# Another opening for a two-layer encoder trunk: x loaded ahead of c, c multiplied as 48 rows in fp32r, and a new order of the work

## The chip, the core and the metric

One Trainium2 chip, one core of it. The metric is the device time in microseconds of one execution of the program. The kernel before has been timed three times: 724.77, 724.97 and 725.40 us; its profiled execution took 725.12 us.

## The reference

Two layers, a sequence of 256 tokens of width 1024, everything in float32. Each layer is modulated by a vector `c`: shift, scale and gate come out of a product with `w_ada` (1024 x 6144). Cut to what matters here:

```python
c_act = jax.nn.silu(c)
for l in range(DEPTH):                                       # 2
    ada = c_act @ w_ada[l] + b_ada[l]
    sh1, sc1, gt1, sh2, sc2, gt2 = split(ada)                # six pieces of 1024
    h = rms(x, g_mix[l]) * (1.0 + sc1) + sh1
    parts = split(h @ w_in[l])                               # 1024 -> 5120
    qa, ka = axial_rope(rms(qa, q_norm_a[l]), ...), ...      # gains per head dimension
    y_a = gqa_attention(qa, ka, va) @ w_branch_a[l]
    y_b = dilated_attention(qs, ks, vs) @ w_branch_b[l]
    x = x + gt1 * ((gate_a * y_a + gate_b * y_b) @ w_out[l])
    h2 = rms(x, g_mlp[l]) * (1.0 + sc2) + sh2
    x = x + gt2 * (square(relu(h2 @ w_ff1[l])) @ w_ff2[l])
```

So before the first product with `w_in` can run, the kernel needs: x, its root mean square and its transpose; silu(c); the first 128 columns of shift and scale, which are rows of `w_ada` reduced against silu(c); and the first 128 rows of `w_in`.

## The kernel before

**Tiling.** x lies in SBUF as two halves of 128 tokens (t = 0, 1). The width 1024 is cut into eight blocks of 128, k = 0 to 7. Weights come as tiles of 128 x 1024 float32 (512 KB) through a ring of seven buffers `wr`. A weight tile is split into two fp32r parts, a high part written by ScalarE (ACT) and the remainder written by VectorE (DVE); so is h. A product is then three fp32r matmuls: high by high, low by high, high by low. A "plain" product is a single float32 matmul on the unsplit tiles, which the profile shows as two MATMUL rows of 512 columns.

**Order of the work.** Instructions are not issued as the code calls them. A class `Plan` records every operation, and at the end plays them through with a table of costs: each engine takes the operation that is due first among those that are ready. `OPEN`, `CFG`, `FIRST`, `COLD`, `FILL` and the like are its constants: `OPEN["loads"]` and `OPEN["steps"]` give the order of loads and of steps in the opening, `OPEN["eng"]` which engine (a for ACT, d for DVE) takes each step's copies and norms, and `seq0` and `seq1` the order in which later pieces are recorded. As all operations are issued by one helper, every row of the profile has the same line; tiles tell them apart.

**The opening** is what is done before and during the products of h with the first 128-row blocks of `w_in`:

- `c_in` holds c as 8 rows of 128 beside an 8 x 8 identity, padded to 128 rows with zeros. `step_c` makes silu(c) (tanh on ACT, a product on DVE), and eight plain float32 matmuls with a picked identity column broadcast each of the 8 rows to all partitions; two ACT copies write `c_act`, 128 x 1024.
- `xin` holds an identity, biases, gains, rotary tables and the two halves of x, loaded by two transfers, x0 and x1.
- `step_a` reduces the first two `w_ada` tiles against `c_act` (DVE, the rows CUSTOM_DVE_ANT_0 of the profile, ISA in the order). `first_sh_sc` then adds bias and gain with two small DVE rows, for each k.
- `step_x` makes the two sums of squares of a half, the power -1/2 on GpSimd (POOL), the normalised half `xn` and its transposes `xT` through PE. `step_t` makes the rotary tables of the first layer on PE.
- `step_h` and `step_m` are the first stage: h of block k = 0, and its products with the tiles `wx` and `wy`, of which `OPEN["plain"]` names those that are plain. Then follow k = 1 to 7 in a loop, each with two `w_ada` tiles, two weight tiles and 24 fp32r matmuls.
- `keep_warm(n)` issues matmuls on a zeroed tile `warm`, n units of 128 columns; `WARM` of them stand first on PE.

Of the kernel before, what the change touches and what calls it, by code (L numbers as in the profile page):

```python
# [12 lines left out]
F32 = mybir.dt.float32  # L13
# [7 lines left out]
P = 128  # L21
D = 1024
# [12 lines left out]
  post0=(5, 2, 1, 0), s2k=9, ahead=1, last="k",  # L35
  hk=2,
  ada_f0=[2, 3, 11, 2, 0, 1, 0, 8, 1], ada_f1=[1, 0, 0, 0, 0, 0, 0, 0, 0],
  seq0="w v v w a w c3 c4 a w w v w a v u a w w w w w u w w w b w b w w v w u w y w w w y w y y w".split(),
  seq1="w u w c4 v w w w w w a w u w c3 w v a a w c5 w w u w w c2 w a w y w y y w y w w u w b w w w b v w v w".split())
WR = 7  # L40
NB8 = 16
WARM = 5
# [4 lines left out]
FIRST = 500.0  # L47
# [6 lines left out]
X0 = 128 + 16 + 128 + 256  # L54
OPEN = dict(
    loads="x0 x1 a0 a1 wx wy",
    steps="C T1 F0 X0 A X1 T0 F1 Wy H0 Wx H1 My0 Mx0 Mx1 My1",
    eng=dict(c0="a", c1="a", ss00="d", ss01="a", ss10="d", ss11="a", xn00="a", xn01="d", xn10="a",
             xn11="a", xT00="a", xT01="a", xT10="d", xT11="a", t00="a", t01="a", t10="a", t11="a",
             h0="d", h1="a", i0="d", i1="a"),  # L60
    plain="y0 y1",
    shift={})
COLD = 5200.0
FILL = (6000.0, 3), (8500.0, 4)
# [92 lines left out]
class Plan:  # L157
# [101 lines left out]
    def record(self, e, op, a, k):  # L259
# [6 lines left out]
        o["also"], o["then"], o["soon"] = [], None, self.soon and e == "SP"  # L266
# [22 lines left out]
    def cost(e, op, outs, ins, k):  # L289
# [18 lines left out]
        if e == "SP":  # L308
# [26 lines left out]
    def links(self):  # L335
        last = {}
        for o in self.ops:
# [6 lines left out]
            for kind, fs in (("r", o["r"]), ("w", o["w"])):  # L344
                for name, space, p0, p1, m in fs:
                    for j, jk, q0, q1, jm in last.get(name, ()):
# [7 lines left out]
                        late = not same or o["e"] == "SP" or (o["e"] != "PE" and kind == "r")  # L354
# [46 lines left out]
    def due(self, seq, at=None):  # L401
# [12 lines left out]
        for o in reversed(self.ops):  # L414
            i = o["i"]
            d = due[i]
            lat = 3500 if o["e"] == "SP" else o["lat"]
# [12 lines left out]
    def run(self, due):  # L430
# [8 lines left out]
        free["SP"] = 0.0  # L439
        pipe = [0.0]  # L440
        dve_port, held_port, last_cut = 0.0, (0.0, 0.0), ""
        chain, pending = False, None
# [34 lines left out]
        def expect(i, depth=0):  # L477
            z = 0.0
            for j, how in ops[i]["need"].items():
                if ops[j]["e"] == "SP":  # L480
                    z = max(z, landed.get(j, 1e18))
                    continue
# [63 lines left out]
        while count < n:  # L546
            moved = False
            for e in ORDERED:
# [15 lines left out]
                if pick is None and seen[e] == state[0] and e not in again:  # L564
                    if e == "DVE" and pending is not None:
                        held_port = enter(*pending, t)
                        pending = None
# [47 lines left out]
                if e == "DVE" and pending is not None and (  # L615
                    pick is None or not chain or not ops[pick]["port"] or ops[pick]["occ"] < 100.0 or t > free[e] + 30.0
                ):
# [18 lines left out]
                if e == "DVE":  # L636
# [4 lines left out]
                    chain = o["port"] and slow == 0.0 and "reduce" not in o["op"]  # L641
                elif e == "POOL":
# [1242 lines left out]
```

## Time and profile before

| What | Before |
|---|---|
| Median of three executions | 724.97 us |
| Profiled execution, its own time | 725.12 us |
| Its span | 723.3 us |
| PE busy | 718.4 us (99%) |
| DVE, ACT busy | 587.6 us (81%), 466.3 us (64%) |
| First matmul on a weight tile | 12.70 us |
| Read from HBM | 178.66 MB |

The profile lists times from the start of the span. A row of the timeline is a run of like instructions on one engine: when the first began, how long the run lasted, what it wrote and read, and in brackets how long the engine had stood idle ahead of it and what ended that. PEld is the loading of weights into the array, which runs beside PE. SPq is the queue from which transfers are issued. In a table of windows each line gives, for a stretch of time, the busy time of the engines and the number of their instructions, then granted clock, share of the DMA engines and GB/s.

### The profile page before, as it was taken

The page shows a single profiled execution, that of the slowest core. Times are in us where ns is not written, and L with a number is a line of the kernel's source. Part 1 is how long each engine was busy: PE and PEld are TensorE (multiplying, and loading weights), DVE is VectorE, ACT ScalarE, POOL GpSimd, SP SyncE. Part 2 cuts the span into 40 slices and gives each one's busy share as a digit, 9 for nine tenths or more (in the row PEclk, how much of TensorE's full clock was granted, in tenths as well). Part 3 has the DMA queues.
Part 4 walks back from the last instruction along what each step waited for, and adds up shares of the span by engine and source line. Part 5 has one row for each costly group of instructions (what it writes and reads, how often), then busy time and mean ns, then how long its engine had stood idle before and what let it go on. Part 6 is the DMA issues. An engine that isn't in the chain of part 4 may idle for free.

```text
span 723.3 us, 10610 instructions
## 1 busy us (share of the span) xinstructions
PE 718.4 (99%) x3860; PEld 597.2 (83%) x3860; DVE 587.6 (81%) x919; ACT 466.3 (64%) x791; POOL 69.6 (10%) x60
## 2 busy tenths in 40 slices
PE   9999999999999999999999999999999999999998
PEld 6788888788888888888888888878788888888887
DVE  6999999999999986594799999797899755456643
ACT  7569678965764766653565598658848766545640
POOL 0007640000100040000032201010000000000000
PEclk9999999999999999999999999999999999999999
DMA  9998668997499997596565687967376965576101
GB/s 349 408 401 270 193 203 295 348 373 243 142 350 406 381 359 278 183 325 233 175 221 207 213 328 269 338 226 280 122 258 199 344 207 159 172 229 211 52 0 59
DMA packets 50868, 180.95 MB, mean 250 GB/s; under 512 B 5728, under 2 KB 6784, under 8 KB 50816
## 3 DMA queue, kind: packets, MB, share of 16 engines
q1 hardware_dynamic: 50816, 180.28, 70.7%
q8 instruction: 30, 0.49, 0.3%
q14 instruction: 22, 0.18, 0.1%
HBM read 178.66 MB, written 1.06 MB: 248 GB/s over the span
## 4 chain that ended last, share of the span: by engine, by line
PE 98%; DMA 1%; SPq 0%; issue 0%; DVE 0%
PE ps L721 98%; DMA wr<-in_w_y 1%; SPq L721 0%; DVE xin L721 0%
## 5 line engine op out<-in xcount | busy, mean ns | idle before, releaser
L721 DVE TENSOR_TENSOR w<-wr,w 128x1024 fp32r<-128x1024 f32 x234 | 282.3, 1229 | 44.7 <-ACT w L721 44.3
L721 ACT ACTIVATE w<-wr 128x1024 fp32r<-128x1024 f32 x234 | 241.5, 1056 | 81.8 <-PE ps L721 38.9
L721 PE MATMUL ps<-w,hT 128*128 128x512 f32 x1032 | 246.4, 395 | 0.0
L721 PEld LDWEIGHTS ps<-w,hT 128*128 128x128 f32 x1032 | 190.3, 188 | 41.5 <-DVE hT L721 1.7
L721 PE MATMUL ps<-w,hid 128*128 128x512 f32 (+1 forms) x780 | 176.0, 385 | 0.0
L721 PEld LDWEIGHTS ps<-w,hid 128*128 128x128 f32 x780 | 143.1, 188 | 28.3
L721 PE MATMUL ps<-hT,w 128*128 128x512 f32 (+1 forms) x896 | 158.5, 337 | 0.0
L721 PEld LDWEIGHTS ps<-hT,w 128*128 128x128 f32 x896 | 139.4, 190 | 18.7
L721 DVE CUSTOM_DVE_ANT_0 s2k<-wr,c_act 128x1024 bf16<-128x1024 f32 x96 | 116.1, 1227 | 0.0
L721 ACT ACTIVATE s2k<-ps 128x256 f32<-128x256 f32 (+3 forms) x108 | 45.4, 440 | 81.0 <-PE ps L721 75.3
L721 DVE TENSOR_TENSOR s2k<-ps,s2k 128x256 f32<-128x256 f32 x56 | 22.8, 419 | 32.5 <-ACT s2k L721 32.5
L721 PE MATMUL ps<-w,mT 128*128 128x512 f32 x192 | 45.6, 393 | 0.0
L721 ACT ACTIVATE s2k<-s2k 128x512 f32<-128x512 f32 (+1 forms) x62 | 38.6, 623 | 9.2 <-DVE s2k L721 8.3
L721 PEld LDWEIGHTS ps<-w,mT 128*128 128x128 f32 x192 | 35.5, 188 | 7.4 <-ACT mT L721 0.2
L721 POOL TENSOR_TENSOR rstd<-rstd,half 128x8 f32<-128x8 f32 (+1 forms) x20 | 30.1, 1509 | 87.8 <-DVE rstd L721 87.7
L721 POOL TENSOR_TENSOR ss<-ss,half 128x1 f32<-128x1 f32 x8 | 11.1, 1383 | 261.7 <-DVE ss L721 254.6
L721 DVE TENSOR_TENSOR hid<-s2k,hid 128x512 fp32r<-128x512 f32 x28 | 20.1, 719 | 19.8 <-ACT hid L721 19.7
L721 ACT ACTIVATE pr<-pr,st 128x256 f32<-128x256 f32 (+1 forms) x64 | 32.3, 558 | 0.8 <-DVE st L721 0.8
L721 DVE TENSOR_TENSOR s2k<-ps,gtb 128x512 f32<-128x512 f32 (+1 forms) x18 | 11.7, 658 | 18.4 <-PE ps L721 18.4
L721 PEld LDWEIGHTS ps<-xin,s2k 128*128 128x128 f32 x180 | 20.9, 141 | 6.3 <-DVE s2k L721 1.2
L721 PE MATMUL ps<-xin,s2k 128*128 128x128 f32 x180 | 26.0, 274 | 0.0
L721 POOL TENSOR_TENSOR s2k<-s2k,tabs 128x256 f32<-128x256 f32 (+1 forms) x20 | 20.2, 1031 | 57.8 <-ACT s2k L721 51.5
(109 smaller groups left out, 505.0 us busy)
## 6 DMA issues: line engine op xcount, KB each, us to landing
wr<-in_w_ff SPq DMA_DIRECT2D x120, 512.0 KB, 4.9
wr<-in_w_ada SPq DMA_DIRECT2D x96, 512.0 KB, 5.7
wr<-in_w_gate SPq DMA_DIRECT2D x32, 512.0 KB, 4.8
wr<-in_w_qkv SPq DMA_DIRECT2D x24, 512.0 KB, 5.3
wr<-in_w_x SPq DMA_DIRECT2D x16, 512.0 KB, 5.2
wr<-in_w_out SPq DMA_DIRECT2D x16, 512.0 KB, 5.3
wr<-in_w_y SPq DMA_DIRECT2D x8, 512.0 KB, 6.7
wr<-in_w_ba SPq DMA_DIRECT2D x8, 512.0 KB, 6.1
```

The costliest lines, as they stand in the source:

```text
L721: getattr(self.real[o["e"]], o["op"])(*map(real, o["a"]), **{n: real(z) for n, z in o["k"].items()})
```

## The change

1. **Loads.** x is issued first on SyncE's queue (SP), with x1 ahead of x0; c is issued from ACT's queue, as its first instruction. x1 carries the columns the first layer's opening needs (biases and gains `early`, head gains, both rotary tables). All other biases and gains are a transfer `small` of 64 KB that is planned near 50 us. The identity is made by GpSimd. The `w_ada` and weight tiles of the first stage come in the order a1, a0, wy, wx in place of a0, a1, wx, wy.
2. **c.** It has 48 rows: 8 rows of c, zeros up to row 32, the 8 rows again, zeros. ACT writes all as fp32r, DVE replaces rows 32 to 47 by the remainder of that rounding, and eight fp32r matmuls over 48 rows take the place of eight plain ones. DVE instead of ACT copies the result to `c_act`.
3. **Modulation.** Bias and gain enter the reduction as its start value and its scale, as columns read from SBUF; the constants 0.5 and 0.0 stood there. Of the two small rows behind each pair one is left (`one_more`).
4. **First stage.** Only wx by the half t = 1 is plain; before, both halves by wy were. PSUM tiles of the stage are allotted where they are first used, not all at once.
5. **Constants and orders.** `WARM` 8 in place of 5, other fills, other planner constants (with a rule for GpSimd's wait on DVE), and new `post0`, `ada_f0`, `seq0`, `seq1`, so that the order differs to the end of the program.

```diff
-  seq0="w v v w a w c3 c4 a w w v w a v u a w w w w w u w w w b w b w w v w u w y w w w y w y y w".split(),
+  seq0="a w v w v w w c4 c3 a w u v w a a w v u w w w w w w b w w b u w w w v y w w y w w w y w y".split(),
-WARM = 5
+WARM = 8
+CR = 48
-    loads="x0 x1 a0 a1 wx wy",
-    steps="C T1 F0 X0 A X1 T0 F1 Wy H0 Wx H1 My0 Mx0 Mx1 My1",
+    loads="x1 x0 a1 a0 wy wx",
+    steps="Wy C X0 X1 T0 T1 F0 A H1 Mx1 F1 H0 Wx My0 Mx0 My1",
-    plain="y0 y1",
+    plain="x1",
-COLD = 5200.0
-FILL = (6000.0, 3), (8500.0, 4)
+COLD = 6650.0
+FILL = (6000.0, 3), (10500.0, 1)
...
+    pool.memset(ident, 0.0)
+    pool.affine_select(
+        out=ident, in_=ident, compare_op=ALU.not_equal, fill=1.0, base=0, pattern=[[-1, P]], channel_multiplier=1
+    )
...
-        dve.tensor_tensor_reduce(junk, raw, c_act, 0.5, 0.0, ALU.mult, ALU.add, col)
+        dve.tensor_tensor_reduce(junk, raw, c_act, *ends(l, w, s, k), ALU.mult, ALU.add, col)
+    def ends(l, w, s, k):
+        ks = slice(k, k + 1)
+        if s < 2 and (l, w) == (0, 0):
+            return (0.5, early[:, 0, ks]) if s == 0 else (early[:, 2, ks], 0.0)
+        return (g_col[:, l, w, ks], 0.0) if s == 1 else (0.5, b_col[:, l, w, s, ks])
+    def one_more(k):
+        sc = shg[0, 0][:, 1, k : k + 1]
+        dve.tensor_tensor(sc, sc, early[:, 1, k : k + 1], op=ALU.add)
-    def first_sh_sc(k):
...
-        dve.tensor_scalar(sc, sc, g_col[:, 0, 0, k : k + 1], gb[:, k : k + 1], op0=ALU.mult, op1=ALU.add)
-        dve.tensor_tensor(sh, sh, b_col[:, 0, 0, 0, k : k + 1], op=ALU.add)
...
     with plan.first():
-        sp.dma_start(c_in, a["c"])
+        act.dma_start(c_in[:CR], a["c"])
...
+        with plan.rush():
+            act.activation(c_sig, z, AF.Tanh, scale=0.5)
+            dve.scalar_tensor_tensor(z, c_sig, 1.0, z, op0=ALU.add, op1=ALU.mult)
+            act.activation(c_f[:CR], c_in[:CR], AF.Copy)
+            dve.tensor_tensor(c_f[low, :P], c_row[low], f32(c_f[low, :P]), op=ALU.subtract)
...
-                    ps[:, k * P : (k + 1) * P], pick[:, kk : kk + 1].to_broadcast([P, P]), c_row,
+                    ps[:, k * P : (k + 1) * P], c_f[:CR, P + kk : P + kk + 1].to_broadcast([CR, P]), c_f[:CR, :P],
...
-    r["x0"] = con(np.concatenate([np.eye(P, dtype=np.float32), b_col, g, g0, g0, cs[0], x[0]], 1))
-    r["x1"] = con(np.concatenate([x[1], cs[1]], 1))
+    r["small"] = con(np.concatenate([b_col, g], 1))
+    r["x0"] = con(x[0])
+    r["x1"] = con(np.concatenate([x[1], b_col[:, :16], g[:, :8], g0, g0, cs[0], cs[1]], 1))
```

SP's queue at the start of the program. Before:

```order
L721 DMA c_in<-in_c 128x136
L721 DMA xin<-in_x 128x1552
L721 DMA xin<-in_x 128x1280
L721 DMA wr_83<-in_w_ada 128x1024
L721 DMA wr_84<-in_w_ada 128x1024
L721 DMA wr_85<-in_w_x 128x1024
L721 DMA wr_86<-in_w_y 128x1024
```

Now:

```order
L723 DMA xin<-in_x 128x1576
L723 DMA xin<-in_x 128x1024
L723 DMA wr_86<-in_w_ada 128x1024
L723 DMA wr_87<-in_w_ada 128x1024
L723 DMA wr_88<-in_w_y 128x1024
L723 DMA wr_89<-in_w_x 128x1024
```

c has left the queue (48 x 136 words of it now stand on ACT's), x has 2600 words a row in place of 2832, and wx is last.

DVE between the sums of squares (`ss`) and the first h (`s2k` out of `xT` and `shg`, which is h of one half). Before:

```order
L721 SCALAR_TENSOR_TENSOR ss_104<-ss_104 128x1
L721 TENSOR_SCALAR s2k_101<-xin,ss_103 128x512
L721 ISA s2k_93,shg_80<-wr_83,c_act 128x1024
L721 ISA shg_80 128x1
L721 ISA s2k_94,shg_80<-wr_84,c_act 128x1024
L721 ISA shg_80 128x1
L721 TENSOR_TENSOR shg_80<-shg_80,xin 128x1
L721 TENSOR_SCALAR shg_80<-shg_80,xin 128x1
L721 TENSOR_SCALAR s2k_98<-xT,shg_80 128x128
```

Now (ss_106 is of the half t = 1, ss_107 of t = 0):

```order
L723 COPY c_act<-ps_76 128x512
L723 SCALAR_TENSOR_TENSOR ss_106<-ss_106 128x1
L723 COPY c_act<-ps_77 128x512
L723 TENSOR_SCALAR s2k_104<-xin,ss_106 128x512
L723 SCALAR_TENSOR_TENSOR ss_107<-ss_107 128x1
L723 ISA s2k_98,shg_83<-wr_86,c_act,xin 128x1024
L723 ISA shg_83 128x1
L723 ISA s2k_99,shg_83<-wr_87,c_act,xin 128x1024
L723 ISA shg_83 128x1
L723 TENSOR_SCALAR s2k_101<-xin,ss_107 128x512
L723 TENSOR_TENSOR shg_83<-shg_83,xin 128x1
L723 TENSOR_SCALAR s2k_102<-xT,shg_83 128x128
```

The copies of `c_act` and a second normalisation (s2k_101) stand among them now; one small row is gone; the reductions read `xin` as well.

PE from the transposes (identity in `xin` before, `ident` now) to the first products with weights (`wr` plain, `w20wx` and `w20wy` split). Before:

```order
L721 MATMUL ps_74<-xin,s2k_95 128x128 x4
L721 MATMUL ps_72<-warm 128x512
L721 MATMUL ps_79<-xin,s2k_96 128x128 x4
L721 MATMUL ps_75<-wr_86,s2k_98 128x512
L721 MATMUL ps_72<-wr_86,s2k_98 128x512
L721 MATMUL ps_76<-w20wx,hT_91 128x512
```

Now:

```order
L723 MATMUL ps_75<-warm 128x384
L723 MATMUL ps_75<-warm 128x128
L723 MATMUL ps_77<-ident,s2k_97 128x128 x2
L723 MATMUL ps_78<-ident,s2k_101 128x128 x4
L723 MATMUL ps_77<-ident,s2k_97 128x128 x2
L723 MATMUL ps_79<-wr_89,s2k_102 128x512
L723 MATMUL ps_82<-wr_89,s2k_102 128x512
L723 MATMUL ps_75<-w20wy,hT_94 128x512
```

The first weight product is with wx in place of wy, and the transposes of s2k_101, which DVE writes behind its two reductions, stand ahead of it.

More of the change, by code (lines that the diff above doesn't have):

```diff
@@ L353, in links @@
                                 continue
-                        late = not same or o["e"] == "SP" or (o["e"] != "PE" and kind == "r")
+                        late = not same or self.ops[j]["dma"] or o["e"] == "SP" or (o["e"] != "PE" and kind == "r")
                         wait(j, 2 if late else 1)
@@ L547, in run @@
             moved = False
+            if pending is not None and t >= pending[1] + 70.0 and dve_port <= pending[1] + 70.0:
+                held_port = enter(*pending, pending[1] + 70.0)
+                pending = None
             for e in ORDERED:
@@ L564, in run @@
                 if pick is None and seen[e] == state[0] and e not in again:
-                    if e == "DVE" and pending is not None:
+                    if e == "DVE" and pending is not None and t >= pending[1] + 70.0:
                         held_port = enter(*pending, t)
@@ L820, in ada_jobs @@
                 for k in range((l, w) == (0, 0), KT):
-                    for s in range(2):
+                    for s in (1, 0) if (l, w) == (0, 0) else (0, 1):
                         ada_tile(l, w, s, k, shg[l, w][:, s, k : k + 1])
-                        if s == 1 and (l, w) == (0, 0):
-                            first_sh_sc(k)
+                        if s == 0 and (l, w) == (0, 0):
+                            one_more(k)
                         if s == 1 and k == KT - 1 and (l, w) != (0, 0):
-                            sh_sc(l, w, 0, KT)
+                            sc = shg[l, w][:, 1]
+                            dve.tensor_tensor(sc, sc, b_col[:, l, w, 1, :], op=ALU.add)
                         yield
@@ L1588, in encoder @@
     c_in = cp.tile([P, P + KT], F32, name="c_in")
-    c_row, pick = c_in[:, :P], c_in[:, P:]
+    c_row, low = c_in[:, :P], slice(32, CR)
+    c_f = cp.tile([P, P + KT], F32R, name="c_f")
     with plan.first():
-        sp.dma_start(c_in, a["c"])
+        act.dma_start(c_in[:CR], a["c"])
     warm = tl("sbuf", [P, 2 * D], F32, "b8", NB8, "warm")[:, :512]
@@ L1648, in step_a @@
     def step_a():
-        for s, raw in enumerate(loaded):
+        gain_first(early[:, 2], early[:, 1])
+        for s, raw in loaded.items():
             junk = s2k(f"aj0{s}", BF16, 1024)
-            dve.tensor_tensor_reduce(junk, raw, c_act, 0.5, 0.0, ALU.mult, ALU.add, v0[:, s, :1])
-        first_sh_sc(0)
+            dve.tensor_tensor_reduce(junk, raw, c_act, *ends(0, 0, s, 0), ALU.mult, ALU.add, v0[:, s, :1])
+        one_more(0)
     def step_w(n):
@@ L1696, in encoder, with q0 @@
     hT = h_tiles(0, 0)
-    pss = {c: [pb(f"q0_{c}_{t}") for t in range(2)] for c in (0, 1, 2, 5)}
+    pss = {}
+    def q0(c, t):
+        if (c, t) not in pss:
+            pss[c, t] = pb(f"q0_{c}_{t}")
+        return pss[c, t]
     h_k0 = {}
@@ L1757, in encoder @@
         if k == KT - 1:
+            with plan.not_before(50000.0):
+                sp.dma_start(small, a["small"])
+            gain_first(g_col, b_col[:, :, :, 1, :])
             with plan.not_before(62000.0):
```

94 lines of the change are left out of this document (43 added, 51 removed).

## The prediction

> **What bounds the kernel now.** I read the busy line first, then the chain of work that ended last, then what TensorE (PE) waited for.
>
> ```profile
> span 723.3 us, 10610 instructions
> PE 718.4 (99%) x3860; PEld 597.2 (83%) x3860; DVE 587.6 (81%) x919; ACT 466.3 (64%) x791; POOL 69.6 (10%) x60
> ```
>
> ```profile
> 4.06 8.51 DMA wr<-in_w_y
> 12.56 0.14 issue
> 12.70 18.07 PE ps L721 x71
> 30.77 0.04 issue
> 30.81 689.44 PE ps L721 x3732
> 720.25 0.02 issue
> 720.27 0.42 DVE xin L721
> ```
>
> ```profile
> PE ps L721 <- DVE half L721: 1.5, 1, 1.5
> PE ps L721 <- DMA wr<-in_w_y: 0.3, 1, 0.3
> ```
>
> PE is the chain from 12.70 us to 720.25 us and waits for nothing in between. Ahead of it stands one transfer, issued at 4.06 and landed at 12.57. So the time is 12.7 us of opening, 707.5 us of PE work, 3 us of tail, and 1.82 us around the span (725.12 for the profiled execution; the median 724.97 is 0.15 lower). As matmul ends are modelled, I checked for hidden gaps in PE's own timeline:
>
> ```profile
> 12.70 1.95 PE L721 MATMUL ps<-wr,s2k 128*128 128x512 f32 x4 [0.31 <-DMA wr<-in_w_y]
> 14.09 3.31 PE L721 MATMUL ps<-w20wx,hT 128*128 128x512 f32 x12
> 17.23 1.88 PE L721 MATMUL ps<-wr,s2k 128*128 128x512 f32 x4
> 18.55 43.77 PE L721 MATMUL ps<-w,hT 128*128 128x512 f32 x187
> ...
> 212.15 11.07 PE L721 MATMUL ps<-w,hid 128*128 128x512 f32 x48
> 223.06 2.20 PE L721 MATMUL ps<-hT,w 128*128 128x512 f32 x9
> ```
>
> In mid-kernel 48 matmuls of 512 columns take 10.91 us, 0.227 each. The 187 of the opening take 43.77, 0.234 each: at most 1.3 us lost over 44 us. That and the 12.7 us ahead are all that this change can win back; the order of the rest can only lose.
>
> **The change, part by part.** The PE instructions behind the opening are the same in number and form (both orders end alike, and the tail's rows answer each other). What can move is the time at which the first matmul on weights starts, the work of the first stage, and the gaps of the steps after it.
>
> *Loads.* The rows that carry the old opening:
>
> ```profile
> 0.74 0.38 SPq L721 DMA_DIRECT2D c_in<-in_c  x1
> ...
> 1.18 0.89 SPq L721 DMA_DIRECT2D xin<-in_x  x2
> ...
> 1.45 2.50 PE L721 MATMUL ps<-warm 128*128 128x512 f32 x4 [1.45 <-DVE half L721]
> ...
> 2.59 0.31 ACT L721 ACTIVATE s2k<-c_in 8x128 f32<-8x128 f32 x1 [0.57 <-DMA c_in<-in_c]
> 2.93 0.28 DVE L721 SCALAR_TENSOR_TENSOR c_in<-s2k,c_in 8x128 f32<-8x128 f32 x1 [1.50 <-ACT s2k L721]
> ...
> 3.75 3.30 PE L721 MATMUL ps<-c_in 128*128 128x128 f32 x16
> ...
> 5.88 0.63 ACT L721 ACTIVATE s2k<-xin 128x512 bf16<-128x512 f32 x1 [2.98 <-DMA xin<-in_x]
> ...
> 6.70 0.69 DVE L721 TENSOR_TENSOR s2k<-s2k,xin 128x512 f32<-128x512 f32 x1
> ...
> 6.88 0.81 PE L721 MATMUL ps<-warm 128*128 128x384 f32 x2
> 7.31 0.15 DVE L721 SCALAR_TENSOR_TENSOR ss<-ss 128x1 f32<-128x1 f32 x1
> ...
> 8.59 0.49 DVE L721 TENSOR_SCALAR s2k<-xin,ss 128x512 f32<-128x512 f32 x1
> 8.99 1.22 DVE L721 CUSTOM_DVE_ANT_0 s2k<-wr,c_act 128x1024 bf16<-128x1024 f32 x1
> ...
> 9.56 1.53 PE L721 MATMUL ps<-xin,s2k 128*128 128x128 f32 x12
> ...
> 10.14 1.22 DVE L721 CUSTOM_DVE_ANT_0 s2k<-wr,c_act 128x1024 bf16<-128x1024 f32 x1
> ...
> 10.93 1.02 PE L721 MATMUL ps<-warm 128*128 128x512 f32 x2
> ...
> 11.28 0.15 DVE L721 TENSOR_TENSOR shg<-shg,xin 128x1 f32<-128x1 f32 x1
> ...
> 11.40 0.27 DVE L721 TENSOR_SCALAR shg<-shg,xin 128x1 f32<-128x1 f32 x1
> 11.78 0.35 DVE L721 TENSOR_SCALAR s2k<-xT,shg 128x128 f32<-128x128 f32 x1
> ...
> 12.04 0.68 DVE L721 COPY xT<-ps 128x512 f32<-128x512 f32 x1
> ```
>
> ```profile
> 8.00:12.50 4.50, 4.39 (x33) 2.82 (x30) 4.11 (x12) 4.20 (x9) 1.11 (x2) 1.00 1.03 421
> 12.50:18.50 6.00, 5.80 (x19) 3.69 (x20) 5.58 (x12) 5.23 (x11) 0.00 (x0) 1.00 1.02 408
> 18.50:24.00 5.50, 5.50 (x24) 4.24 (x23) 5.47 (x11) 3.13 (x5) 0.00 (x0) 1.00 1.03 410
> ...
> 30.00:36.00 6.00, 5.96 (x26) 4.42 (x25) 5.91 (x11) 3.58 (x6) 0.00 (x0) 1.00 1.03 409
> ```
>
> The stream runs full (DMA share 1.02 to 1.03, last column some 410 GB/s). With x first on SP it begins at 0.74 instead of 1.18: 0.44 earlier. By the last weight of the stage it has 1300 KB of x (128 rows of 1576 and 1024 words) ahead instead of 1484 KB of c and x (136, 1552 and 1280 words), and 25 KB of c from ACT's queue beside them: 0.16 MB less at 410 GB/s is 0.40. So the first half of x (now x1, 12 KB larger than x0 was) is there at 5.88 - 0.44 + 0.03 = 5.45, each 512 KB tile 1.28 later (x0 6.7, a1 8.0, a0 9.3), and the last weight at 12.57 - 0.84, some 11.8. Were PE still waiting for that weight, it would start 0.8 earlier.
>
> *It will not, since DVE's queue takes its place.* Followed in the new order, with start-to-start times of the rows above: x1 at 5.45; table diagonal, gains (0.07, 0.61, 0.07, 0.07) to 6.3; copy of c_act's first half, new on DVE, by the COPY row under 0.68, start to start 0.60, to 6.95; sum of squares (ACT's two squares took 0.63 each, done at 6.8) to 7.1; GpSimd's power, 1.13 from the end of that row (7.46) to its users (8.59), to 8.25; normalisation 0.40 (8.59 to 8.99) to 8.65; second half's sum 0.08; two reductions 1.14 each to 11.0; the other half's normalisation, 0.49, to 11.5; then six transposes stand on PE ahead of the first weight matmul: (10.93 - 9.56) / 12 = 0.114 each (the warm-up behind them starts at 10.93), 0.7. That gives 12.25. The modulated rows (sum 0.15, scaling 0.35) are ready at 12.0, the weight at 11.8; both are hidden.
>
> *Reductions with two operands from SBUF.* Scale or start value of each reduction is now a column and not a constant; no row shows this form. Below: nothing. Above: the 128x1 TENSOR_SCALAR with two columns takes 0.27, the TENSOR_TENSOR of the same size 0.15, so 0.12. One column of the two: I take 0.06, or 12.37 for the start; the ends are 12.25 and 12.5. In return the 0.27 row per step goes away. As DVE is busy 5.47 of 5.5 us in the steps that follow, the balance there is -0.27 + 2 x 0.06, a gain of 0.15 per step that ends no wait, as PE itself is full: zero.
>
> *c.* tanh 0.31, product 0.28, and two new rows (fp32r copy, remainder) costed like these: 1.35 from landing to c_f with the hand-overs. It must be ready by about 5.4 to leave the copy at 6.35 alone, so c must land by 4.0. Below: 2.56, as before (tanh at 2.59). Above: behind all of x1, 5.4, as before x came behind c on one queue. c has three rows on each of 16 engines against eight of x1, which favours the early end: I take 3.5, hidden by the warm-up, which now ends near 5.0 (1.45 us start, 8 units of 128 columns in place of 5). The Trainium skill, page "DMA: Bandwidth & Descriptors", section "Queues, rings and completion order", says that an engine takes turns between queue rows packet by packet; by that c lands near 3 and costs nothing, by the in-order row it costs what the second rival costs. The old trace has loads on one queue alone, so it shows neither.
>
> *First stage.* One plain group of 4 rows and 12 fp32r matmuls take 17.23 - 12.70 = 4.53, so a plain pair is 4.53 - 12 x 0.227 = 1.81. Before: two such pairs and 12 matmuls, 6.34. Now one pair and 18, 5.90: 0.44 less. ACT's copies and DVE's remainders in the new order come 0.1 late once (the low part of h for the second half follows a reduction of 1.14); I add 0.1. The identity on GpSimd is done before x lands, the bias and gain columns come with x1, `small` is issued near 50 us in place of nothing: no cost.
>
> **Sum:** start -0.33, first stage -0.44, late row +0.10: -0.67. The profiled execution would be 724.45, the median 724.3.
>
> **The rivals.**
>
> 1. *The gaps of the opening go too.* For: DVE is the fullest engine there and loses a row per step; up to 1.3 us stand in the 187 matmuls, some 0.4 of it the hand-over from plain matmuls. Against: ACT waits for landings there, and PE and the stream both move by the same 0.7. With 0.8 more gone: 723.5.
>
> 2. *c lands behind x1.* c_f at 6.8, first half of c_act's matmuls at 7.5, the copy at 7.5 instead of 6.35; everything behind it moves by 1.15, the start to 13.5. Then the change does not do what it says: -0.44 + 0.10 + 0.8 = +0.5, 725.4. Against it: three rows against eight on each engine.
>
> 3. *The slower side: columns cost the reductions more.* Place: DVE in the seven steps of the opening, 5.91 busy of 6. The point is 0.14 each, where two of them eat the 0.27 that was saved. If a column costs as much as that whole 0.27 row, each step grows by 0.27, seven by 1.9, and the start goes to 12.8, +0.1: with -0.44 and +0.1 for the first stage that makes +1.65, 726.6. For it: DVE has no slack there. Against: a pair of columns cost 0.12 in the row measured.
>
> 4. *PE's clock.* Before, the 16 c matmuls of 128 columns start 0.196 apart on the mean (3.75 to 6.88), the 12 transposes of the same size 0.114: PE ran at about half rate until near 6.9, though the granted clock reads 1.00 throughout. In the new order PE has 0.9 us of work (warm-up of 384 and of 128 columns, by the 6.88 row 0.65 and a third of it) between the second transposes, near 9.5, and the last, from 11.5. If that brought the half rate back for as long as it lasted at first (from 1.45), 5.3 us at half rate, 2.6 are lost: 726.9. Against: no row of the old trace shows the half rate come back. The Trainium skill, "TensorE: Matmul & The Clock Gate", Part 1, has the clock fall after an idle window of about 3.4 us; by that rule the gap here is too short, and nothing in the old trace speaks against it.
>
> **How the numbers follow.** Forecast 0.60, rivals in order 0.18, 0.11, 0.07, 0.04. The time is that of the likeliest, 724.3. The forecast's own ends: start 12.25 to 12.5, and half of the 1.3 us of gaps won or added again, 723.6 to 725.1. To leave out no more than two in ten, the range takes in rival 1 and 2: 723.2 to 725.6. About 0.2%, 1.45 us, is what a measurement of this kernel tells from no change. Below 723.5: most of rival 1 and an edge of the forecast, 0.18. Above 726.4: rivals 3 and 4 for the most part, 0.09. Within: 0.73.
>
> **What would show it.** Right: first weight matmul of PE near 12.4, with DVE's second normalisation and the transposes just ahead, the weight's landing some 0.5 us earlier; the second step's matmuls beginning near 18.3 behind fp32r matmuls; PE without waits to the end. Wrong: a reduction longer than 1.28 us; c's tanh after 4 us with a hole in PE near 5; transposes 0.2 us apart after 10 us; the 512-column matmuls of the opening more than 0.24 or less than 0.23 apart; PE waiting anywhere past 60 us, which would say that the new order of the rest costs something that this sum leaves out.

## The result, and the profile after

The changed kernel takes 726.40 us (median of 21 executions), the kernel before 724.97 (21 executions in turn with them on the same chip, 724.71 to 725.40). One of the 21 took 1860.97 us and is left out of all that follows; the other 20 lie between 725.30 and 727.93, with a median of 726.30. The ratio is 1.0020, with a 95% interval of 1.0013 to 1.0027: slower by about what can be told from no change, where 724.3 was forecast. The profiled execution took 726.40, 1.28 more than that of before.

The busy lines of the page after:

```profile
span 724.6 us, 10624 instructions
PE 718.7 (99%) x3854; PEld 595.9 (82%) x3854; DVE 590.7 (82%) x907; ACT 469.4 (65%) x795; POOL 69.2 (10%) x62
```

What PE waited for, after (engine, tile, what ended the wait; total, times, longest):

```profile
PE ps L723 <- DVE half L723: 1.5, 1, 1.5
PE ps L723 <- DVE c_f L723: 1.1, 1, 1.1
PE ps L723 <- DVE s2k L723: 0.2, 1, 0.2
```

The wait for the last weight is gone, and one for c has come. The timeline of the opening, after:

```profile
0.73 0.42 ACTq L723 DMA_DIRECT2D c_in<-in_c  x1
0.74 0.86 SPq L723 DMA_DIRECT2D xin<-in_x  x2
...
1.45 3.60 PE L723 MATMUL ps<-warm 128*128 128x512 f32 x4 [1.45 <-DVE half L723]
...
4.86 0.31 ACT L723 ACTIVATE s2k<-c_in 48x128 f32<-48x128 f32 x1 [2.40 <-DMA c_in<-in_c]
...
5.83 0.63 ACT L723 ACTIVATE s2k<-xin 128x512 bf16<-128x512 f32 x1
5.87 0.28 DVE L723 TENSOR_TENSOR c_f<-c_in,c_f 16x128 fp32r<-16x128 f32 x1 [0.38 <-ACT c_f L723]
...
6.20 1.11 PE L723 MATMUL ps<-c_f 48*128 48x128 f32 x8 [1.15 <-DVE c_f L723]
...
7.27 0.68 DVE L723 COPY c_act<-ps 128x512 f32<-128x512 f32 x1
...
8.69 0.49 DVE L723 TENSOR_SCALAR s2k<-xin,ss 128x512 f32<-128x512 f32 x1
...
9.16 1.28 DVE L723 CUSTOM_DVE_ANT_0 s2k<-wr,c_act,xin 128x1024 bf16<-128x1024 f32 x1
...
9.90 1.88 PE L723 MATMUL ps<-ident,s2k 128*128 128x128 f32 x8
...
11.57 0.48 DVE L723 TENSOR_SCALAR s2k<-xin,ss 128x512 f32<-128x512 f32 x1
11.62 1.03 PE L723 MATMUL ps<-warm 128*128 128x384 f32 x4
...
12.49 1.04 PE L723 MATMUL ps<-ident,s2k 128*128 128x128 f32 x8
...
13.36 1.88 PE L723 MATMUL ps<-wr,s2k 128*128 128x512 f32 x4
...
19.44 38.49 PE L723 MATMUL ps<-w,hT 128*128 128x512 f32 x168
```

Two things stand out. The tanh of c begins at 4.86 (before: 2.59), and PE is idle for 1.15 us until c_f is there at 6.20. And the eight transposes at 9.90 take 1.88 us where the eight at 12.49 take 1.04: PE ran at half rate once more. The windows view says so itself (the engines stand in the order PE, PEld, DVE, ACT, POOL). After:

```profile
1.40:4.70 3.30, 3.25 (x4) 1.18 (x4) 0.17 (x2) 1.06 (x1) 0.00 (x0) 1.00 0.74 248
4.80:8.10 3.30, 2.15 (x17) 1.65 (x18) 2.42 (x9) 2.89 (x9) 0.00 (x0) 1.00 1.01 412
8.20:11.50 3.30, 3.30 (x18) 2.22 (x15) 3.23 (x6) 2.38 (x6) 1.98 (x2) 0.50 1.02 411
11.60:15.00 3.40, 3.40 (x19) 2.21 (x17) 2.86 (x9) 3.26 (x7) 0.00 (x0) 1.00 1.04 413
```

The granted clock is 0.50 from 8.15 to 11.57, one record of 3.41 us; the full clock had been granted at 4.74, and the record ahead of the fall holds the hole. The column reads 1.00 also where the trace has no record, as ahead of 4.74, so it shows a fall, not the first grant; I read that from the first record and from the spacing of the matmuls. In the profile of before the full clock was granted once, at 6.57.

The mean granted clock of every execution is on record too. A record of 3.41 us at half takes 0.0024 off it (3.41 x 0.5 / 724.6). It is 0.997 or 0.998 in seven of the 20 executions, which lie between 725.98 and 726.80 us, the profiled one among them. It is 1.000 in the five fastest (725.30 to 725.65) and also in the four slowest (727.54 to 727.93). So what made the slowest ones late was not a fall of this kind. A first grant that comes late would not show in this mean, as time ahead of it counts as full; that it was this is likely, not shown.

To place the time I cut both traces at the same points of the program: the first matmul on a weight tile, the first matmul on the second block (plus 0.41 in the kernel before, where its row begins while the last plain row still runs), the first matmul behind the opening's eight blocks, and the last matmul.

| us | Before | After | Difference | Forecast |
|---|---|---|---|---|
| Start of the weight matmuls | 12.70 | 13.36 | +0.66 | -0.33 |
| First stage | 6.26 | 6.08 | -0.18 | -0.34 |
| Seven steps to the end of the opening | 38.79 | 38.69 | -0.10 | 0 |
| The rest, to the last matmul | 662.20 | 663.07 | +0.87 | 0 |
| Sum | 719.95 | 721.20 | +1.25 | -0.67 |

So half of the miss lies in the first 13 us, and nearly half behind the opening, where the forecast had nothing. Behind the opening both traces hold the same number of PE rows of every form, as the prediction said; the 0.87 is lost in when they run.

### The profile page after: what moved, and what is told of

Same layout as the page of the kernel before. It is cut to its first block, busy times and chain, and to the rows that moved or that the text cites. A ratio compares the mean times of both kernels' runs of the same rounds, so it can differ in the third digit from the quotient of the medians.

```text
span 724.6 us, 10624 instructions
## 1 busy us (share of the span) xinstructions
PE 718.7 (99%) x3854; PEld 595.9 (82%) x3854; DVE 590.7 (82%) x907; ACT 469.4 (65%) x795; POOL 69.2 (10%) x62
## 4 chain that ended last, share of the span: by engine, by line
PE 93%; DVE 3%; ACT 2%; DMA 1%; issue 1%; ACTq 0%; DVEq 0%
PE ps L723 93%; DVE s2k L723 2%; DMA wr<-in_w_ada 1%; DVE w L723 1%; DMA c_in<-in_c 1%; ACT s2k L723 0%; ACT hT L723 0%; ACT w L723 0%; DVE rstd L723 0%; ACT xT L723 0%; ACT tabs L723 0%; ACT w20wx L723 0%; DVE shg L723 0%; DVE xin L723 0%; ACT c_f L723 0%
## 5 line engine op out<-in xcount | busy, mean ns | idle before, releaser
L723 DVE CUSTOM_DVE_ANT_0 s2k<-wr,c_act,small 128x1024 bf16<-128x1024 f32 x80 | 101.3, 1278 | 5.2 <-DMA wr<-in_w_ada 5.2
L723 PEld LDWEIGHTS ps<-ident,s2k 128*128 128x128 f32 x180 | 21.5, 145 | 6.5 <-DVE s2k L723 1.5
L723 PE MATMUL ps<-ident,s2k 128*128 128x128 f32 x180 | 26.8, 281 | 0.0
```

The costliest lines, as they stand in the source:

```text
L723: getattr(self.real[o["e"]], o["op"])(*map(real, o["a"]), **{n: real(z) for n, z in o["k"].items()})
```

## The experiments

Fifteen kernels; all but two of them compute the same. Diffs are cut to the lines that matter. Where an edit is made at the place where the planned operations are issued, the planned order stays as it was. "Opening ends" and "rest" are the cuts of the table above, from one profiled execution each.

### What in the opening: c's queue, the hole, the clock

**c ahead of x on SP's queue**, all else as changed:

```diff
-  getattr(self.real[o["e"]], o["op"])(...)
+  e = "SP" if o["op"] == "dma_start" else o["e"]
+  getattr(self.real[e], o["op"])(...)
```

> The changed kernel with one thing undone: c (still 48 rows) is issued by SP ahead of x and not by ACT beside it; every engine's order is otherwise kept. Theory 1 (c lands late, at 4.84 us, PE stands idle 1.15 us and its clock falls back to half for one window, 8.15 to 11.57): c's tanh near 2.7 us, no hole in PE near 5, no half-clock window, first weight matmul near 12.7 in place of 13.36, time near 725.6 and runs within 0.8 us of each other. Rival (the reductions with a column operand, 1.28 us in place of 1.22, hold DVE back): start 0.1 to 0.2 earlier at most, 726.2. Third (the new order of the rest loses 0.9 us behind 58 us): that loss stays in both.

Measured: 725.89 (725.28 to 727.04, 11 executions), ratio 1.0014 (1.0005 to 1.0022). c's tanh began at 2.45 and PE had no hole of note, but the first full clock came only at 9.66, so that the table matmuls ran at half rate:

```profile
5.16 1.97 PE L724 MATMUL ps<-c_f 48*128 48x128 f32 x8
6.78 3.44 PE L724 MATMUL ps<-s2k,xin 64*128 64x128 f32 x16
10.15 1.09 PE L724 MATMUL ps<-ident,s2k 128*128 128x128 f32 x8
```

Start 13.03, opening ends 57.53, rest 662.96. c early takes away the wait; it does not by itself fix when the clock is granted. A spread within 0.8 us had been expected; it was 1.76. The loss behind the opening stayed, as expected.

**One warm-up matmul of 512 columns more**, c late as changed:

```diff
+  if warmed == 2:        # PE's second matmul is issued twice
+      getattr(self.real[o["e"]], o["op"])(...)
```

> The changed kernel with one more warm-up matmul of 512 columns behind the first two, all else kept, so that PE is busy for 0.85 us of the 1.15 us in which it waits for c. Theory 1, its part on the clock: no half-clock window after the first grant, transposes 0.11 and not 0.22 us apart, first weight matmul near 13.0, time near 726.0, the spread of runs (725.3 to 727.9) narrower. If the lateness of c alone decides and not the clock: start unchanged at 13.3, 726.4. Rival (reductions): unchanged, 726.4.

Measured: 725.96 (725.70 to 726.17, 11 executions), ratio 1.0012 (1.0004 to 1.0021). The full clock was granted once, at 6.68, and the spread fell from 2.6 to 0.5 us; but c's matmuls, ready at about 6.2, stood behind the longer warm-up until 6.81, and the start came at 13.06.

**Both edits together:**

> The changed kernel with c's load ahead of x on SP's queue and one more warm-up matmul of 512 columns, order kept. Theory (two separate losses in the opening, c's late landing and the clock that falls back): c's tanh near 2.5, no hole in PE ahead of the matmuls on c, clock granted once before 7.5, start 12.5 to 12.8, opening ends 57.0 to 57.3, rest 663.0 as in the changed kernel, time 725.2 to 725.6 with a spread under 0.6. Rival (one loss only): as good as the better of the two edits alone, 725.9.

Measured: 726.08 (725.02 to 726.78, 11 executions), ratio 1.0013 (1.0004 to 1.0021); start 13.28, opening ends 57.69. The expectation that the two gains add up fell: with c early, the longer warm-up itself held c's matmuls back, from 5.16 to 6.87. The spread was 1.76 us where under 0.6 was expected, although PE has no hole of note here: five executions lie between 725.02 and 725.49, six between 726.08 and 726.78.

**The kernel before, with only c's load moved to ACT's queue** (8 rows of c, padded to 128, the old order):

```diff
+  e = "ACT" if o["op"] == "dma_start" and o["i"] == self.c_load else o["e"]
```

> The kernel before, with one thing of the change: c's load (8 rows) is issued on ACT's queue instead of ahead of x on SP's, every other row in the old order. Theory (ACT's queue begins late): c's first packet starts some 1.8 us after its issue and c lands at 4.4 to 4.9 instead of 2.56, x lands at most 0.1 earlier than 5.86, the 16 plain matmuls on c begin near 5.9 instead of 3.75 with a hole in PE ahead of them, the start of the weight matmuls moves from 12.70 to between 13.0 and 13.8, the time to 725.3 to 726.1, and the granted clock has more than one record. Rival (turns alone decide, and in the changed kernel it was c's 48 rows that made it late): c at 3.0 to 3.6, x 0.4 earlier, start 12.2 to 12.5, time 724.5 to 724.8.

Measured: 728.40 (728.30 to 729.00, 5 executions), ratio 1.0049 (1.0035 to 1.0063): far more than either theory gave. The chain of waits of this kernel:

```profile
0.74 5.39 DMA c_in<-in_c
6.13 0.02 issue
6.15 0.32 ACT s2k L722
6.47 0.02 issue
6.50 0.29 DVE c_in L722
6.79 0.04 issue
6.83 716.66 PE ps L722 x3856
```

c landed at 6.13, not at 4.4 to 4.9. The old load has 128 rows, eight on each of the 16 engines, as many as x0 has; the new one has 48, three on each, and landed at 4.84. (6.13 - 4.84) / 5 is 0.26 for one more row, the time in which an engine moves a row of x and one of c (0.24 and 0.03 us in the steady part of the trace). So c and x do take turns row by row. The Trainium skill, "DMA: Bandwidth & Descriptors", section "Queues, rings and completion order", has the engines take turns between queue rows packet by packet: the trace agrees. What the forecast lacked is when these turns begin and when the last engine ends them. The first row on ACT's queue moved at 2.55 in the changed kernel and at 2.02 here, the first on SP's at 1.76 and 1.75. In the changed kernel the 16 engines then ended their shares of c one after the other, from 3.51 to 4.50 (by the 16 packets of 4 bytes behind c's 48 rows), and c landed behind the last. Why ACT's queue begins later isn't shown. In this kernel the hole was 2.9 us, the full clock came at 11.99 and the start at 16.49; the rest took 662.20, as before. An opening late by 3.8 us thus costs 3.2 at the end, and nothing behind it.

**The hole filled**, by five warm-up matmuls of 128 columns behind the first two:

```diff
+  if warmed == 3:
+      for _ in range(5):
+          pe.matmul(cold[:, :P], warm[:, :P], warm[:, :P], start=True, stop=True)
```

> The changed kernel with five warm-up matmuls of 128 columns more behind the first two, order kept: some 1.05 us of PE work at half rate, which fills the hole of 5.05 to 6.20 without making the matmuls on c later than their data. Theory (the hole is what lets the clock fall back): one record of granted clock, from 8.3 at the latest, transposes 0.114 apart behind it, start 12.5 to 12.9, opening ends 57.1 to 57.5, rest 663.0, time 725.2 to 725.8 with a spread under 0.8. Rival (c's late landing costs by itself, through the copies of c_act): start 13.0 to 13.4, opening ends 57.6 to 58.1, time 725.9 to 726.4.

Measured: 725.58 (725.15 to 726.49, 11 executions), ratio 1.0011 (1.0002 to 1.0020). The expectation had a wrong size: a plain float32 matmul is two rows on PE, so five are ten rows of 0.2 (2.3 us), and c's matmuls came at 7.30. The median still fell by 0.8. The profiled execution was one of the late ones (726.41, clock granted at 7.68, start 13.73).

**The same with two of them:**

> The changed kernel with two warm-up matmuls of 128 columns more (four rows of 0.2, 0.85 us), which end near 5.9 where the hole ended at 6.2. Order kept. Theory (the hole is what makes the clock fall back or come late): matmuls on c at 6.2 as before, one record of granted clock, start 12.4 to 12.9, rest 663.0, median 725.2 to 725.6, below the 725.58 with the longer fill. Rival (the clock's grant falls where it will): median 725.9 to 726.4, spread over 1.5.

Measured: 725.33 (725.04 to 727.12, 11 executions), ratio 1.0009 (1.0000 to 1.0018): 1.07 less than the changed kernel (0.97 less than the median of its 20), by four rows of PE work that compute nothing. Its rows:

```profile
4.97 0.61 PE L729 MATMUL ps<-warm 128*128 128x128 f32 x4
6.11 1.11 PE L731 MATMUL ps<-c_f 48*128 48x128 f32 x8 [0.53 <-DVE c_f L731]
...
9.13 1.09 PE L731 MATMUL ps<-ident,s2k 128*128 128x128 f32 x8
...
12.72 1.88 PE L731 MATMUL ps<-wr,s2k 128*128 128x512 f32 x4
```

And its windows, over the same stretches as above:

```profile
4.80:8.10 3.30, 2.77 (x23) 2.15 (x23) 2.51 (x9) 2.95 (x10) 0.10 (x1) 1.00 1.01 407
8.20:11.50 3.30, 2.80 (x20) 1.73 (x16) 3.23 (x8) 2.89 (x6) 1.89 (x2) 1.00 1.03 417
```

c is as late as before, and the clock, granted once at 4.91, stayed: transposes at 9.13 take 1.09 for eight, the start is 12.72, and the opening ends at 57.17 instead of 58.13. So the profiled execution of the changed kernel lost 0.64 at the start and 0.96 by the end of the opening against this one, most of it through the clock. Two of eleven executions still lay above 726, against 14 of 20 in the changed kernel, so the fill makes the loss rarer; it does not end it. Five executions of the changed kernel itself, those of 725.30 to 725.65 whose clock did not fall, lie where this median does.

### What behind the opening: columns or order

**All reductions with constants**, in the changed kernel (this leaves out gain and bias of the modulation; the other reductions on DVE get the constants 0.5 and 0.0 in place of their own too):

```diff
+  if o["op"] == "tensor_tensor_reduce":
+      a[3], a[4] = 0.5, 0.0
```

> The changed kernel with the constants 0.5 and 0.0 as scale and start of every reduction, as before the change; gain and bias so enter no modulation (that part of the computation is left out). Orders kept. Rival (columns cost 0.06 us in each of 96 reductions, 16 of them in the opening, on the path there): reductions 1.22 us, first weight matmul 0.12 earlier, steps of the opening at 5.45 without the 5.8 of the last, 0.5 to 0.9 us off the time: 725.6. Theory 1: 0.1 to 0.2 at most, 726.2, as PE is full in those steps.

Measured: 727.23 (724.67 to 727.50, 7 executions), ratio 1.0020 (1.0009 to 1.0031). The time says little: the profiled execution had the clock late (first grant 13.67, start 15.30), and five of the seven lie between 726.27 and 727.50, two at 724.67 and 725.41. Its rest is what the run was for: 662.52 instead of 663.07.

**The old tables behind the new opening** (`post0`, `ada_f0`, `seq0`, `seq1` of before):

```diff
-  post0=(5, 2, 0, 1), s2k=9, ahead=1, last="k",
+  post0=(5, 2, 1, 0), s2k=9, ahead=1, last="k",
...
```

> The changed kernel with the old table that orders the work behind the opening (post0, ada_f0, ada_f1, seq0, seq1); the opening's order is the same up to the last step. Third theory (the new order loses 0.9 us behind the opening: last step's end to last matmul 663.07 in place of 662.2): 662.3, time 725.6. Theories 1 and 2: the loss behind the opening comes from the reductions or from the state in which the opening leaves the engines, so it stays: 726.4.

Measured: 730.58 (729.19 to 731.59, 5 executions), ratio 1.0071 (1.0057 to 1.0085); start 12.77, opening ends 57.21, rest 668.28. The old tables do not fit the changed planner and the changed rows, so this run cannot say what the new order costs against the old one in its own kernel.

Its trace says more on the clock. Its opening is that of the changed kernel, with c as late (tanh at 4.81) and a hole of 0.92 us ahead of c's matmuls. But the full clock was granted at 5.77, in the middle of that hole, and did not fall: PE was busy 2.87 of 3.41 us ahead of the grant and 2.94 behind it. So the opening ended at 57.21 without any filling. The clock fell later, at 63.80, behind two waits of 0.53 and 1.20 us that lie in one stretch of 3.41 us:

```profile
60.39:63.80 3.41, 1.68 (x9) 0.98 (x8) 3.34 (x8) 3.27 (x8) 3.20 (x4) 1.00 0.03 9
63.80:67.21 3.41, 3.41 (x10) 2.58 (x9) 3.38 (x6) 3.41 (x8) 3.33 (x4) 0.50 0.75 240
```

Some 1.7 of the 6.1 us that this kernel's rest is longer are this record at half (an estimate: half of 3.41). Cut into stretches of 3.41 us from the first grant on, the traces with clock records (all but one) hold no other fall ahead of the last matmul. The least busy stretch that kept the clock is 75%, in two kernels; this is the one of the kernel with c first and constants (below):

```profile
4.48:7.89 3.41, 2.57 (x21) 1.80 (x22) 1.97 (x7) 2.04 (x7) 0.12 (x1) 1.00 0.99 372
```

A hole may also put off the first grant. In the kernel with all reductions constant, above, the stretch from 3.43 on, in which PE was busy 2.38 of 3.41 us, did not bring it, nor did the next, which c's and the tables' matmuls fill; it came only at 13.67. That execution took 727.26 us and has a mean clock of 1.000, like the slowest of the changed kernel.

**The kernel before, with a column as the scale of the reductions.** The first version gave a column to all 114 reductions on DVE, and so changed the scale of two sums of squares and of the softmax's 16 as well, whose values then were others:

```diff
+  if o["op"] == "tensor_tensor_reduce":
+      a[3] = self.col              # a column that holds 0.5
```

> The kernel before, with one thing of the change: the 80 reductions take their scale from a column of SBUF that holds 0.5 and not from a constant (one memset on GpSimd more), old order kept. Theory (a column costs each reduction 0.05 to 0.06 us, and behind the opening this ends waits of PE): reductions 1.28 instead of 1.22, start 12.70 to 12.80, the rest behind the opening 662.2 + 0.5, the time 725.4 to 725.8. Rival (DVE has slack behind the opening, so the 0.87 that the changed kernel lost there is its order's): rest 662.2 to 662.3 and time 724.9 to 725.1.

Measured: 727.58 (727.50 to 727.78, 5 executions), ratio 1.0037 (1.0024 to 1.0049), rest 664.52. The second version changes the 96 reductions over c_act alone:

> The kernel before, in which only the 96 reductions over c_act take their scale from a column of SBUF (holding 0.5) instead of a constant; the 18 other reductions, which the earlier version of this experiment changed too (its softmax and two of its sums of squares, so that their values were others), keep their constants. Old order. Theory (96 times 0.06 us on DVE ends waits of PE behind the opening): reductions 1.28 to 1.29, start 12.4 to 12.8, rest 663.0 to 664.2 instead of 662.2, time 725.7 to 727.0. Rival (the 2.3 us of the earlier version came from the 16 reductions of the softmax, 0.6 us each, which PE waits for): rest 662.2 to 662.7, time 724.9 to 725.5.

Measured: 727.08 (726.83 to 727.43, 6 executions), ratio 1.0030 (1.0019 to 1.0042), start 12.64, opening ends 57.95, rest 663.95. The group of its reductions, and that of the changed kernel behind the opening and in it (the last two numbers are busy us and mean ns; before, 96 took 116.1 us, 1227 each):

```profile
L725 DVE CUSTOM_DVE_ANT_0 s2k<-wr,c_act,col 128x1024 bf16<-128x1024 f32 x96 | 122.0, 1289 | 0.2 <-DMA wr<-in_w_ada 0.2
```

```profile
L723 DVE CUSTOM_DVE_ANT_0 s2k<-wr,c_act,small 128x1024 bf16<-128x1024 f32 x80 | 101.3, 1278 | 5.2 <-DMA wr<-in_w_ada 5.2
L723 DVE CUSTOM_DVE_ANT_0 s2k<-wr,c_act,xin 128x1024 bf16<-128x1024 f32 x16 | 20.3, 1279 | 0.0
```

A column costs 0.05 to 0.06 us a reduction, and in the old order some 5 us of it on DVE (80 reductions behind the opening) lengthened the rest by 1.75 us, although PE is the bound. The windows behind the opening of the kernel before say why:

```profile
57.00:110.00 53.00, 53.00 (x280) 43.42 (x280) 52.45 (x87) 43.08 (x87) 34.00 (x29) 1.00 0.68 216
110.00:190.00 80.00, 80.00 (x532) 64.81 (x531) 77.78 (x135) 58.79 (x114) 1.47 (x1) 1.00 0.86 305
190.00:480.00 290.00, 290.00 (x1481) 243.70 (x1480) 247.88 (x377) 188.13 (x317) 29.55 (x21) 1.00 0.76 272
430.00:445.00 15.00, 15.00 (x92) 12.57 (x91) 14.86 (x25) 11.93 (x25) 3.27 (x2) 1.00 0.79 298
```

DVE, the third engine of a row, is busy 52.45 of 53 us and 77.78 of 80, and again 14.86 of 15 near 440 us: there a longer DVE row has no slack to hide in. Matched matmul by matmul, counted back from the end, the kernel with columns loses 1.0 of its 1.75 up to 170 us and 0.55 near 440. The changed kernel loses 0.6 of its 0.87 ahead of 182 us and the last 0.2 between 470 and 506.

**Constants behind the opening, computing the same** (the first 16 reductions keep their columns), with the filled hole in one kernel and c first in the other:

```diff
+  tensor_tensor_reduce(junk, raw, c_act, 0.5, 0.0, ALU.mult, ALU.add, col)
+  # at a set's end: v += b; v[:, 1] = (v[:, 1] + 1) * g; gate: c += b
```

> The same, and every reduction behind the opening's first 16 has constants again: seven additions and scalings on DVE (three pairs and four rows of 128x8 or 128x16) take the place of the columns, put in where the set of a layer ends; everything else in the changed kernel's order. Theory (columns cost 0.5 of the rest): opening as in the kernel with the filled warm-up, rest 662.4 to 662.7, time 724.7 to 725.3. Rival (the columns behind the opening are hidden, and the rest is its order's): rest 662.9 to 663.2, time as that kernel's.

> The changed kernel with c's load ahead of x on SP's queue (as in the run that issued c first) and the constants behind the opening, order kept. Theory: opening as in that run, ends 57.0 to 57.6, rest 662.4 to 662.7, time 725.2 to 725.6, its spread as wide as that run's (725.3 to 727.0), since the clock's grant is not fixed by it. Rival (c early is all that was wrong): rest 663.0 and time 725.9.

Measured: 727.60 (727.26 to 728.58, 5 executions) and 728.05 (726.85 to 728.57, 5 executions), ratios 1.0039 (1.0027 to 1.0052) and 1.0040 (1.0027 to 1.0054). Both are slower through my own edit: I had put the gate's addition just ahead of the transposes of the gate, where it stood behind longer rows on DVE and PE waited for it. The waits of PE in the first:

```profile
PE ps L821 <- DVE gcol L820: 1.4, 2, 0.7
```

Its rest was 665.46, that of the second 665.86. The opening of the second, with c early, ended at 57.02 from a start at 12.58. With the addition right behind the set's last reduction, and two filling matmuls in place of five:

> The changed kernel with c's load ahead of x on SP's queue, and constants in every reduction behind the opening's first 16; the row that adds the gate's bias now stands right behind the set's last reduction, not ahead of the transposes on TensorE. Order kept. Theory (columns cost 0.5 of the rest, and c early lets the opening end where it was forecast): opening ends 57.0 to 57.6, rest 662.4 to 662.7, no wait of PE for a gate column over 0.3, time 724.6 to 725.3. Rival (the 0.55 that the run with constants gave back came from the rows it left out): rest 662.9 to 663.2 and time 725.4 to 726.

> Both: c on ACT's queue as in the change, the hole filled by two warm-up matmuls of 128 columns, constants behind the opening. Theory: the median of the fill with two, less 0.5: 724.7 to 725.2, no more than before; rest 662.4 to 662.7. Rival: rest 662.9 to 663.2, time that of the fill with two.

Measured: c first 725.31 (724.75 to 726.34, 11 executions), ratio 1.0004 (0.9995 to 1.0013), rest 662.61; filled 725.09 (724.66 to 726.82, 11 executions), ratio 1.0007 (0.9998 to 1.0016), rest 662.67. Against the same kernels with columns (662.96 and 663.03) that is 0.35 and 0.36 less: the share of the columns in the changed order, net of the small rows that replace them. Expected had been 0.5. In the filled kernel four of the eleven executions lie above 726. Neither kernel differs measurably from the one before.

**The order worked out anew for constants**, with c first and the longer warm-up:

> The same two edits, and behind the opening the old constants in the reductions, with the old rows that add the bias and scale by the gain at the end of a layer's set; the order is worked out anew. Theory (columns cost 0.5 of the rest): opening as in the kernel with the two edits, 57.0 to 57.3, reductions behind it 1.22 to 1.23, rest 662.3 to 662.6, time 724.7 to 725.1. Rival (the order of the rest costs it): rest 662.9 to 663.2 and time 725.2 to 725.6.

Measured: 725.98 (725.68 to 726.30, 11 executions), ratio 1.0014 (1.0005 to 1.0023); start 12.47, opening ends 57.06, rest 663.50. The constants were back (1215 ns each), and the rest still grew: the planner's new order lost more than the rows gained. So 0.45 of the 0.87 (662.65 against 662.20) stays with the changed order and the rows around it. Which of its moves costs it isn't shown.

## Why the prediction was wrong

It was wrong in sign: -0.67 was forecast, +1.25 came. Three of its steps failed. The order and the columns behind the opening were put at nothing and cost 0.87. x was to be there 0.44 earlier and was 0.05 earlier. c was to land at 3.5, hidden by the warm-up; it landed at 4.84, PE stood idle for 1.15 us, the clock fell, and the first weight matmul began at 13.36 where 12.37 was forecast. Taken by its own steps:

- **What bounds the kernel**: right. PE is the chain, and what it waits for sets the time. The step that failed is in the sentence "the order of the rest can only lose" and the cost of zero given to it all the same: it lost 0.87.
- **Loads, "0.44 earlier"**: wrong, the first step that failed. x1 was used from 5.83 where 5.45 was forecast and x0 had been used from 5.88: 0.05 was won. The stream does not run at its full rate from the first issue: in both traces the first row moves at 1.74 to 1.76, whichever load it is of, and c's rows ahead of x, which moved from 1.74 to 2.22, fell into that slow stretch. The windows at the very start, of before and of after:

```profile
0.70:2.70 2.00, 1.25 (x2) 0.73 (x3) 0.51 (x2) 1.40 (x2) 0.00 (x0) 1.00 0.36 72
2.70:4.70 2.00, 2.00 (x8) 1.48 (x8) 0.28 (x1) 0.19 (x1) 0.00 (x0) 1.00 0.95 356
```

```profile
0.70:2.70 2.00, 1.25 (x2) 0.73 (x3) 0.66 (x3) 1.28 (x1) 0.50 (x2) 1.00 0.28 45
2.70:4.70 2.00, 2.00 (x3) 0.44 (x2) 0.00 (x0) 0.00 (x0) 0.00 (x0) 1.00 0.95 364
```

  Up to 2.7 us the last columns read 72 and 45 GB/s, behind it 356 and 364. The forecast took its rate from windows that begin at 8 us.
- **"DVE's queue takes its place"**: right as a mechanism, and its chain can be followed row by row: second normalisation from 11.57 to 12.05 where it was to end at 11.5, mostly the 0.38 of x1. (Its terms add up to 12.16; the prediction rounded up to 12.25 on the way.) With the clock kept (two filling matmuls) the start is 12.72, 0.35 past the forecast's 12.37; of the other 0.64 in the 13.36, DVE's second normalisation brings 0.10 (11.47 there, 11.57 here) and the clock 0.54: the first eight transposes start 0.21 apart instead of 0.11, so that the short warm-up and the last transposes stand late on PE.
- **Columns, 0.06 each**: right in size (1.28 for 1.22), wrong in reach. "A gain that ends no wait" was worked out for the steps of the opening, and holds there. The 80 reductions behind it were not priced; they cost 0.35 in the changed order, 1.75 in the old.
- **c, "I take 3.5"**: wrong. It landed at 4.84, within the bounds given (2.56 to 5.4), past the limit of 4.0 that the step named, and the hole near 5 with a late tanh is what the last part said would show it. The turns were right. What was missing is the start of ACT's queue, 0.8 behind SP's, and the last engine, which ended its share 1 us after the first. Its direct price, through the copy of c_act, was small (start 12.44 and 12.72 with c late and two filling matmuls, 12.49 and 12.58 with c first); its price was the hole in PE. The queues of the changed kernel, from 0.7 to 2.5 us and then from 2.5 to 4.1, by when ACT's had moved 59 of its 64 packets (packets, MB, share of the 16 engines; q1 is SP's, q10 ACT's, which had been issued to at 0.73):

```profile
q1 hardware_dynamic: 14, 0.09, 26.1%
```

```profile
q1 hardware_dynamic: 72, 0.45, 69.0%
q10 hardware_dynamic: 59, 0.03, 17.5%
```

- **First stage**: right in direction, 0.18 instead of 0.34. The stage of before took 6.26, not the 6.34 worked out, and the new one 6.08 (6.11 to 6.18 in the kernels with c first or the hole filled), so that the late rows cost 0.18 or more instead of 0.10.
- **Rival 1, gaps**: partly true. 168 matmuls take 38.49 us, 0.229 each instead of 0.234; with the clock kept the seven steps take 38.32, 0.47 less than before. Therefore those kernels end the opening at 56.90 to 57.20, about the forecast's 57.08, on other terms: a later start and fewer gaps.
- **Rival 4, the half rate**: the right mechanism, given 0.04, at the wrong place. I looked for it behind the second transposes; it came from the hole ahead of c's matmuls, 3 us earlier. The price of 2.6 was too high for the profiled execution (0.96). That the slowest execution, 727.93, is 2.6 above the fastest is luck: its clock did not fall. The half rate that the prediction read "until near 6.9" ended at 6.57 by the clock's record. I leaned on the rule of the Trainium skill ("TensorE: Matmul & The Clock Gate", Part 1) that the clock falls after an idle window; here PE was busy 2.15 of 3.30 us in the stretch ahead of the fall. The measurement decides: a window that is a third idle was enough, and one that is a quarter idle was not. That the window is about 3.4 us long and free-running agrees: both records at half are 3.41 long, and the first grant lies between 4.43 and 13.67 in executions of kernels with like warm-ups. Where the hole falls in that window decides what it costs: in one window it cost the clock (the changed kernel), parted by the window's edge it did not (the kernel with the old tables).

In sum for the medians: +0.87 behind the opening (0.35 of it columns), some -0.55 in the opening when the clock is kept (57.17 to 57.20 against 57.75), and 1.07 for the clock, which is 1.4 of the 1.43 measured (with the median of the 20 in place of all 21: 0.97 for the clock, 1.3 of 1.33). It adds cuts of single profiles to differences of medians, so it is rough. The last term rests on the medians with and without the filled hole; which record is granted in a given execution, and why c's or the tables' matmuls at half the array's rows sometimes do and sometimes don't bring the grant (9.66 in one kernel, 13.67 in another), stays open.

## What to carry to other kernels

An instruction that no longer waits is not the only thing to price: a hole in TensorE can cost its clock, if enough of it falls into one window of 3.41 us, so work that fills a hole without delaying its successor pays although it computes nothing, and work that delays it does not. A few hundredths of a microsecond on each of a hundred rows of another engine reached the end here where that engine was 97% busy or more, even in a kernel in which TensorE is 99% busy; look at the stretch, not at the mean share of 81%. Rates read from the steady stream say nothing of the first two microseconds, and a load on a second queue has a start of its own and lands with its slowest engine.

## What the runs showed of the hardware that I had not expected

- The granted clock fell to 0.50 for one record of 3.41 us after a stretch in which PE was busy 66% (2.26 of 3.41, the changed kernel) and after one of 49% (1.68 of 3.41, the kernel with the old tables), and stayed after two of 75% (2.57 of 3.41). Two falls; what lies between 66% and 75% no run shows.
- The time of one and the same program spread by 0.7 us in the kernel before and by 0.5 with the longer warm-up alone, by 2.6 in the changed kernel with the hole, and by 1.8 with c first, where PE has no hole of note either. So a hole is not the only source of the spread; the rest of it stays open.
- A load issued on ACT's queue at 0.73 or 0.74 moved its first row between 2.02 and 2.76 in the nine kernels that do so; SP's queue moved its first at 1.74 to 1.76 in every kernel. c issued first on SP's queue had landed by 2.59, 128 rows and all.
- Each row more that a load has on an engine, in turn with another load's row of some 6 KB, put its landing back by 0.26 us.
- A reduction whose scale or start value is a column of SBUF takes 1.28 us where the same with constants takes 1.22.
